# A hybrid encoder layer on one core: where near-key attention, residual sums and norm products are done

## The chip, the cores and the metric

One core of a Trainium2 chip runs the whole program. TensorE (PE in the profile; PEld its weight loads) multiplies, VectorE (DVE), ScalarE (ACT) and GpSimd (POOL) work element by element, and SyncE (SP) issues nearly all DMA transfers from one queue, in order. Every engine runs its own instructions in program order and waits on semaphores for the others. The metric is the device time of the program in microseconds; a profiled execution also gives a trace of every instruction. This kernel's runs differ by about 0.3%.

## The reference

One inference step of an encoder layer for 2048 prompt positions and 32 sample positions with a cache of 2048. Cut to what matters:

```python
h = rms_norm(x, g_norm1) * (1 + scale1) + shift1
q, k, v, z, xbc_raw, dt_raw = split(h @ w_in)
attn = stick_breaking(q, k, v)            # 8 heads: weights are beta_j times the product of
attn = rms_norm(attn, g_attn_out)         # (1 - beta) over the keys between j and the query
ssm = ssd_mixer(z, xbc_raw, dt_raw, ...)  # conv, SiLU, chunked scan, rms_norm
x = x + gate1 * (concat([attn, ssm]) @ w_out)
h2 = rms_norm(x, g_norm2) * (1 + scale2) + shift2
x = x + gate2 * ((silu(h2 @ w_gate) * (h2 @ w_up)) @ w_down)
```

with d_model 1024, FFN width 2816, all in float32. Further outputs are keys, values, and the final conv and scan states of prompt and sample.

## The kernel before

Every float32 product is made of two float32r halves, so a matrix is split into a high and a low part (`split`: ScalarE copies, another engine subtracts), and each block takes three matmuls (`mm3`, lines 130 to 132). Weights come by DMA in 1 MB tiles; ScalarE makes `wh`, GpSimd makes `wl`. `Pieces` fetches and splits one tile ahead of its use.

The 2048 positions go in four quarters of 512. The first phase (to about 985 us) projects them, runs the scan, and beside the last projection runs the attention of quarter 0 (`attn`). `scan` is its core: two sigmoids on ScalarE, masks on GpSimd, a running product on VectorE (`tensor_tensor_scan`), and the product `bv` with it (line 237), whose result TensorE transposes. At the end of that phase `ssm_out` and `conv_out` transpose the states, copy them and store them.

The second phase has `Wout`, the output projection of a quarter: `ssm()` adds the mixer's half, `run()` loads the attention's result (`rows`, from `aoD`), multiplies, and for each block of 128 rows makes the second norm (`norm2`). `product` scales the PSUM result by the row's rstd and the gate into `tm` (line 761) and adds it to `x1` (line 763); ScalarE then sums squares of `x1`. `norm2` takes the power -1/2 on GpSimd, scales `xn` on VectorE, transposes it on TensorE, applies scale and shift to the half blocks `hx` (hf 0 on ScalarE, four copies; hf 1 on VectorE, two operations), splits them into two-deep buffers `hl`, and stores these to `h2D`, from where the FFN of that quarter loads its input `h`.

Attention of quarters 1 to 3 looks at near keys only (`attn_w`, 8 heads a quarter, two scans a head); the few queries whose product has not vanished by then are redone over all far keys (`far_keys`).

The order is made by generators, whose yields carry a cost in ns. `merge2(main, side, ratio)` runs the main one and takes from the side one until its costs reach ratio times the main's. `merge2(w0.run(), a1, R2, fin=False)` so puts attention of quarter 1 beside the projection of quarter 0. Then `merge(streamA(), streamF(), 1.9)` interleaves two streams: A does the rest of the near-key attention, the far keys, and projections 1, 2, sample and 3; F does the FFN of the four quarters, in pieces of 96 gate and up matmuls and 48 down matmuls (`pg`, `pu`, `py`). For each cost unit of A, 1.9 of F are taken, and 4.0 once projection 1 is done. F may not load quarter g's input before A has yielded `("done", g)`. A scheduler in the build then moves instructions within this order where it expects engines to wait; what came out of it is shown with the change.

Tile names: `Q`, `Kw`, `Vw` are loads of `attn_w`, `z` scores or a projection's PSUM, `t` transposes, `o` attention results, `ao` an attention result on its way to or from `aoD`, `d` the PSUM of projection 0.

Of the kernel before, what the change touches and what calls it, by code (L numbers as in the profile page):

```python
# [9 lines left out]
AF = mybir.ActivationFunctionType  # L10
ALU = mybir.AluOpType
# [4 lines left out]
P = 128  # L16
# [9 lines left out]
SQ = 1  # L26
EPS = 1e-6
BIG = -1e30
R1, R2 = 1.6, 0.5
T2 = 4  # L30
CC = 3
NE = 4
# [3 lines left out]
def body(tc, nc, I, O):  # L36
    V, A, G, PE = nc.vector, nc.scalar, nc.gpsimd, nc.tensor
    ctx = ExitStack()
    with ctx:
# [169 lines left out]
        def scan(at_, aT, z, n, dd, first, end, mask, ns=2):  # L209

            a = aT[acnt[0] % len(aT)]
            acnt[0] += 1
            nb = abuf[0]
            b = at_.tile([P, 2, 256], F32, tag="b", name="b", bufs=nb)
            bv = b[:, :ns, :n]
            A.activation(a[:, :ns, 256 - n:256], z, AF.Sigmoid, scale=-1.0)
            A.activation(bv, z, AF.Sigmoid)
            av = a[:, :ns, 256 - n:256]
            if mask is not None:
                pat, np_ = mask  # L220
                for p0 in range(0, P, np_):
                    for t, fill in ((av, 1.0), (bv, 0.0)):
                        t = t[p0:p0 + np_]
                        G.affine_select(out=t, in_=t, pattern=pat, compare_op=ALU.is_gt, fill=fill, base=0, channel_multiplier=1)
            if first:
                V.memset(dd[:, :, 256:257], 1.0)
            Pt = at_.tile([P, 2, 257], F32, tag="P", name="Pt", bufs=2)
            if n == 256:
                fl = lambda t: t.rearrange("p a b -> p (a b)")[:, ::-1]
                V.tensor_tensor_scan(fl(Pt), fl(a), fl(dd), 0.0, op0=ALU.mult, op1=ALU.add)  # L230
            else:
                for i in range(ns):
                    r = lambda t: t[:, i, 256 - n:257][:, ::-1]
                    V.tensor_tensor_scan(r(Pt), r(a), r(dd), 0.0, op0=ALU.mult, op1=ALU.add)
            if not end:
                V.tensor_copy(dd[:, :ns, 256:257], Pt[:, :ns, 256 - n:257 - n])
            V.tensor_tensor(bv, bv, Pt[:, :ns, 257 - n:257], op=ALU.mult)
            return b

        def sums(stat, sq, hp, n):  # L240
# [476 lines left out]
        class Wout:  # L717
# [30 lines left out]
            def product(self, hf, r):  # L748

                mH, mL = mHL  # L750
                wh, wl = self.pf.get()
                for b, c, m in self.tb:
                    ps = self.psum()
                    tm = self.tile("tm", "tm")
                    if self.s == 0:
                        mm3(ps[:m], [(mH[:, k, c:c + m], mL[:, k, c:c + m], wh[:, k, :], wl[:, k, :]) for k in range(4)])
                    else:
                        mm2(ps[:2 * DEC], [(mH[:, k, :2 * DEC], wh[:, k, :], wl[:, k, :]) for k in range(4)])
                        fold(tm, ps, 512)
                        ps = tm  # L760
                    V.scalar_tensor_tensor(tm[:m], ps[:m], r[:m, b:b + 1], self.gr[hf][:m], op0=ALU.mult, op1=ALU.mult)
                    x1 = self.x1[hf, b]
                    V.tensor_tensor(x1[:m], x1[:m], tm[:m], op=ALU.add)
                    yield b, tm
                    yield 12 * 216

# [42 lines left out]
            def norm2(self, b, c, m):  # L809
                s, t0 = self.s, self.t0  # L810
                xs = [self.x1[hf, b] for hf in range(2)]
                ss = self.ss[b]
                V.tensor_tensor(ss[:m, 0:1], ss[:m, 0:1], ss[:m, 1:2], op=ALU.add)
                rs = sm.tile([P, 1], F32, tag="rsd", name="rsd")
                rstd(rs[:m], ss[:m, 0:1], 1.0 / D, EPS)
                xn = [self.tile("xn", "xn") for _ in range(2)]
                for hf in range(2):
                    V.tensor_scalar(xn[hf][:m], xs[hf][:m], rs[:m], None, op0=ALU.mult)
                    store(x1D[t0 + c:t0 + c + m, hf * 512:(hf + 1) * 512], xs[hf][:m])
                yield 1300  # L820
                for hf in range(2):
                    ps = tps()
                    pv = ps[:, :4 * m].rearrange("p (k t) -> p k t", k=4)
                    for k in range(4):
                        PE.transpose(pv[:, k, :], xn[hf][:m, k * P:(k + 1) * P], ident[:m, :m])
                    v4 = lambda t: t.rearrange("p (k t) -> p k t", k=4)[:, :, :m]
                    hx = v4(self.tile("tm", "hx"))
                    ksl = slice(hf * 4, hf * 4 + 4)
                    if hf == 0:
                        for k in range(4):  # L830
                            A.activation(hx[:, k, :], pv[:, k, :], AF.Identity, scale=A2[:, k, s:s + 1], bias=mods[:, 24 + k, s:s + 1])
                    else:
                        V.tensor_tensor(hx, pv, A2[:, ksl, s:s + 1].to_broadcast([P, 4, m]), op=ALU.mult)
                        V.tensor_tensor(hx, hx, mods[:, 24 + hf * 4:28 + hf * 4, s:s + 1].to_broadcast([P, 4, m]), op=ALU.add)
                    hl = [v4(self.tile(x, "hl", F32R)) for x in ("hh", "ll")]
                    split(hl[0], hl[1], hx)
                    for i in range(2):
                        store(h2D[i, ksl, :, t0 + c:t0 + c + m].rearrange("k p t -> p k t"), hl[i].bitcast(F32))
                    yield 450
# [205 lines left out]
        with ExitStack() as pa:  # L1045
# [525 lines left out]
            merge2(pr(2, "xz"), rest, 0.6, fin=False)  # L1571
            merge2(pr(2, "qv"), ssd_q(2), 0.68)
            merge2(chain(make_h(3, hH, hL), pr(3, "xz")), rest, 0.6)
            merge2(pr(3, "k"), ssd_q(3), 1.2)
            q = 3
            while klag:
# [5 lines left out]
            V.tensor_copy(mrT[:96], ps[:96, :P])  # L1582
            store(modD.rearrange("m s c -> (m s) c"), mrT[:96])
            ssm_out(st["S"], O["ssm_prompt"])
            ssm_out(st["Sx"], O["ssm_sample"])
            conv_out(carry, O["conv_prompt"])
            conv_out(sconv, O["conv_sample"])
            pr_.close()


# [11 lines left out]
        with ExitStack() as pb_:  # L1602
            mp = pb_.enter_context(tc.tile_pool(name="mp", bufs=1))
            mHL, stat = mixed(mp)
            pw0 = ExitStack()
            w0 = Wout(0, pw0.enter_context(tc.tile_pool(name="wo0", bufs=1)), dense_ps)
            w0.pre()
            merge2(a0, w0.ssm(), R1)
            pa0.close()
            fc = px_.enter_context(tc.tile_pool(name="fc", bufs=1, side="right"))  # L1610
            far_consts(fc)
            L = fc.tile([P, NH, 12], F32, name="L")
            px1 = ExitStack()
            at1 = px1.enter_context(tc.tile_pool(name="at1", bufs=1, side="right"))
            wt = window_tiles(at1)
            a1 = chain(*(attn_w(g, at1, L, wt) for g in range(1, NQ)))
            merge2(w0.run(), a1, R2, fin=False)
            pw0.close()
            fp = pb_.enter_context(tc.tile_pool(name="fp", bufs=1))
            late = {}  # L1620

            def streamA():
                yield from a1
                yield from far_keys(at1, wt[0], L)
                px1.close()
                for g in range(1, NQ):
                    if g == 3:
                        yield from part_s()
                    with tc.tile_pool(name=f"wo{g}", bufs=1, side="right") as wo:
                        yield from project(g, wo)  # L1630
                    if g < 3:
                        yield ("done", g)
                    if g == 1:
                        yield ("ratio", 4.0)
                px_.close()
                late["ex"] = pb_.enter_context(tc.tile_pool(name="ex", bufs=1, side="right"))
                dpool[0] = pb_.enter_context(tc.tile_pool(name="pdF", bufs=5, space=PSUM))
                yield ("done", 3)

            def streamF():  # L1640
                hT = load_h(0, fp, None)
                for g in range(NQ):
                    hT = yield from ffn(g, fp, late, hT)

            merge(streamA(), streamF(), 1.9)


        fx = ctx.enter_context(tc.tile_pool(name="fx", bufs=1))
# [39 lines left out]
def merge2(main, side, ratio, fin=True):  # L1688

    debt = 0.0  # L1690
    for c in main:
        debt += c * ratio
        while side is not None and debt > 0:
            try:
                debt -= max(next(side), 1)
            except StopIteration:
                side = None
    if side is not None and fin:
        for _ in side:
            pass  # L1700
# [58 lines left out]
```

## Time and profile before

| | us |
|---|---|
| three runs | 2985.84, 2990.13, 2994.29 (median 2990.13) |
| the profiled execution, device time | 2991.05 |
| its span, first to last instruction | 2989.3 |
| TensorE busy | 2741.2 (92%) |
| VectorE busy | 1630.7 (55%) |
| GpSimd busy | 1437.8 (48%) |
| ScalarE busy | 1165.4 (39%) |
| DMA | 466.53 MB, mean 156 GB/s |

Busy is the union of an engine's instructions. Matmuls are pipelined: one of 512 columns is listed with 0.39 us, but the next may start 0.23 us later, so it is the steps between starts that count. The granted clock is 1 at 2.4 GHz and 0.5 at 1.2 GHz, and a mean in between tells how much of a stretch ran at which. A wait is given with the instruction after it, its length and what released it.

### The profile page before, as it was taken

To read this page: it belongs to the slowest core of one execution; us is meant where nothing else is said; L and a number is where in the kernel's file an instruction comes from. 1 tells how busy PE (TensorE), PEld (TensorE's weight loads), DVE (VectorE), ACT (ScalarE), POOL (GpSimd) and SP (SyncE) were. 2 spreads that over 40 slices of the span, in tenths; PEclk is the share of its full clock that TensorE was granted. 3 is DMA by queue.
4 is the path that set the end of the run, shared out by engine and by line. 5 is a ranking of instruction groups with operands and counts; after the bars stand their busy time and mean duration, and the time that the engine had idled before them with its cause. 6 is when DMAs were issued, how large, how long until landed. Compare 5 with 4: busy or idle time off the path is not lost.

```text
span 2989.3 us, 41722 instructions
## 1 busy us (share of the span) xinstructions
PE 2741.2 (92%) x15467; PEld 2344.7 (78%) x15467; DVE 1630.7 (55%) x2690; ACT 1165.4 (39%) x2465; POOL 1437.8 (48%) x1237
## 2 busy tenths in 40 slices
PE   6998998988868679998989799999999999999998
PEld 4887997887867668887768588777788778899997
DVE  6577586756567667853445535435634432333336
ACT  6456465545444445522124233323232322322221
POOL 4667566564643435543126233544533545644445
PEclk8999999999988779999989899999999999999999
DMA  8755654363467696647644824444733462422221
GB/s 266 232 160 156 192 172 125 106 198 93 126 177 228 174 267 174 182 132 206 208 156 146 270 91 146 141 137 128 253 116 113 123 199 90 145 90 89 87 85 65
DMA packets 415618, 466.53 MB, mean 156 GB/s; under 512 B 34191, under 2 KB 330991, under 8 KB 415406
## 3 DMA queue, kind: packets, MB, share of 16 engines
q1 hardware_dynamic: 414478, 463.61, 51.5%
q8 instruction: 124, 2.03, 0.3%
q14 instruction: 88, 0.72, 0.1%
q10 hardware_dynamic: 896, 0.14, 0.0%
q0 software_dynamic: 32, 0.03, 0.0%
HBM read 372.66 MB, written 91.04 MB: 155 GB/s over the span
## 4 chain that ended last, share of the span: by engine, by line
PE 57%; DMA 7%; DVE 6%; POOL 2%; issue 2%; ACT 1%; SPq 1%; DVEq 0%; ACTq 0%; POOLq 0%
PE pg L131 5%; PE pu L131 5%; PE pu L130 5%; PE pu L132 5%; PE pg L130 5%; PE pg L132 5%; PE py L130 5%; PE py L131 4%; PE py L132 4%; PE d L132 2%; PE d L130 2%; PE d L131 2%; DMA Kf<-KT 1%; PE z L131 1%; PE z L130 1%
## 5 line engine op out<-in xcount | busy, mean ns | idle before, releaser
L60 POOL TENSOR_TENSOR wl<-wr,wh 128x512 fp32r<-128x512 f32 x752 | 1018.6, 1386 | 1033.9 <-ACT wh L59 947.1
L59 ACT ACTIVATE wh<-wr 128x512 fp32r<-128x512 f32 x816 | 449.8, 620 | 518.6 <-PE py L132 103.5
L130 PE MATMUL d<-wh,hH 128*128 128x256 f32 (+2 forms) x1088 | 313.6, 288 | 20.4 <-ACT hH L59 13.4
L130 PE MATMUL pg<-h,wh 128*128 128x512 f32 (+1 forms) x880 | 312.2, 355 | 16.5 <-DMA h<-h2D 16.5
L130 PE MATMUL pu<-h,wh 128*128 128x512 f32 (+1 forms) x880 | 312.4, 355 | 7.1 <-DVE sg L955 7.1
L132 PE MATMUL d<-wh,hL 128*128 128x256 f32 (+2 forms) x1088 | 309.1, 285 | 7.6 <-POOL hL L60 7.6
L131 PE MATMUL pg<-h,wh 128*128 128x512 f32 (+1 forms) x880 | 310.9, 353 | 1.6 <-DMA h<-h2D 1.6
L132 PE MATMUL pu<-h,wl 128*128 128x512 f32 (+1 forms) x880 | 311.7, 354 | 0.0
L131 PE MATMUL pu<-h,wh 128*128 128x512 f32 (+1 forms) x880 | 311.1, 354 | 0.0
L132 PE MATMUL pg<-h,wl 128*128 128x512 f32 (+1 forms) x880 | 310.7, 353 | 0.0
L131 PE MATMUL d<-wl,hH 128*128 128x256 f32 (+2 forms) x1088 | 308.6, 284 | 0.0
L130 PE MATMUL py<-wh,aH 128*128 128x512 f32 x704 | 285.1, 405 | 16.9 <-DVE ya L986 13.0
L131 PE MATMUL py<-wl,aH 128*128 128x512 f32 x704 | 280.0, 398 | 0.0
L132 PE MATMUL py<-wh,aL 128*128 128x512 f32 x704 | 268.6, 399 | 7.2 <-DVE aL L60 7.2
L986 DVE TENSOR_TENSOR ya<-py,ya 128x512 f32<-128x512 f32 x288 | 190.6, 685 | 127.7 <-PE py L132 125.3
L955 DVE TENSOR_TENSOR sg<-pg,sg 128x512 f32<-128x512 f32 (+1 forms) x110 | 64.9, 590 | 357.2 <-ACT sg L954 357.2
L130 PEld LDWEIGHTS d<-wh,hH 128*128 128x128 f32 (+1 forms) x1088 | 205.0, 188 | 24.4 <-ACT hH L59 14.9
L132 PEld LDWEIGHTS d<-wh,hL 128*128 128x128 f32 (+1 forms) x1088 | 204.3, 188 | 9.0 <-POOL hL L60 8.2
L131 PEld LDWEIGHTS d<-wl,hH 128*128 128x128 f32 (+1 forms) x1088 | 204.7, 188 | 0.9
L960 DVE TENSOR_TENSOR sg<-pu,sg 128x512 f32<-128x512 f32 (+1 forms) x110 | 65.0, 591 | 245.7 <-PE pu L132 244.4
L130 PEld LDWEIGHTS pg<-h,wh 128*128 128x128 f32 x880 | 166.1, 189 | 41.3 <-issue 15.9
L130 PEld LDWEIGHTS pu<-h,wh 128*128 128x128 f32 x880 | 166.5, 189 | 31.4 <-DVE sg L955 8.2
(435 smaller groups left out, 5758.1 us busy)
## 6 DMA issues: line engine op xcount, KB each, us to landing
wr<-in_w_in SPq DMA_DIRECT2D x48, 1024.0 KB
wr<-in_w_gate SPq DMA_DIRECT2D x44, 1024.0 KB
wr<-in_w_up SPq DMA_DIRECT2D x44, 1024.0 KB
wr<-in_w_down SPq DMA_DIRECT2D x44, 1024.0 KB
wr<-in_w_ada SPq DMA_DIRECT2D x24, 1024.0 KB
wr<-in_w_out SPq DMA_DIRECT2D x20, 1024.0 KB
h2D<-hl SPq DMA_DIRECT2D x64, 256.0 KB
Kw<-KT SPq DMA_DIRECT2D x48, 320.0 KB
```

Of the source, the lines that this page charges most:

```text
L59: A.activation(h, src, AF.Copy)
L60: (eng or V).tensor_tensor(l, src, h.bitcast(F32), op=ALU.subtract)
L130: PE.matmul(out, lhsT=sh, rhs=mh, start=(i == 0), stop=False)
L131: PE.matmul(out, lhsT=sh, rhs=ml, start=False, stop=False)
L132: PE.matmul(out, lhsT=sl, rhs=mh, start=False, stop=(i == n - 1))
L955: V.tensor_tensor(sg[:, :n], pg[:, :n], sg[:, :n], op=ALU.mult)
L960: V.tensor_tensor(sg[:, :n], pu[:, :n], sg[:, :n], op=ALU.mult)
L986: V.tensor_tensor(dst, ps[:r], dst, op=ALU.add)
```

## The change

Six edits. In `scan`, the last product goes to GpSimd in every other call. In `product`, the sum onto `x1` goes from VectorE to GpSimd. In `norm2`, ScalarE applies scale and shift to both half blocks. The sample's scan state and both conv states are put out before the key projection of quarter 3, not after it. Projection 0's `run()` is written alone, and the attention of quarter 1 is left to stream A. The ratio of the streams is 1.55 for 1.9 (until projection 1 is done; 4.0 after that stays).

```diff
-            V.tensor_tensor(bv, bv, Pt[:, :ns, 257 - n:257], op=ALU.mult)
+            (G if acnt[0] % 2 else V).tensor_tensor(bv, bv, Pt[:, :ns, 257 - n:257], op=ALU.mult)
...
-                    V.tensor_tensor(x1[:m], x1[:m], tm[:m], op=ALU.add)
+                    G.tensor_tensor(x1[:m], x1[:m], tm[:m], op=ALU.add)
...
-                    if hf == 0:
-                        for k in range(4):
-                            A.activation(hx[:, k, :], pv[:, k, :], AF.Identity, scale=A2[:, k, s:s + 1], bias=mods[:, 24 + k, s:s + 1])
-                    else:
-                        V.tensor_tensor(hx, pv, A2[:, ksl, s:s + 1].to_broadcast([P, 4, m]), op=ALU.mult)
-                        V.tensor_tensor(hx, hx, mods[:, 24 + hf * 4:28 + hf * 4, s:s + 1].to_broadcast([P, 4, m]), op=ALU.add)
+                    for k in range(4):
+                        kk = hf * 4 + k
+                        A.activation(hx[:, k, :], pv[:, k, :], AF.Identity, scale=A2[:, kk, s:s + 1], bias=mods[:, 24 + kk, s:s + 1])
...
+            ssm_out(st["Sx"], O["ssm_sample"])
+            conv_out(carry, O["conv_prompt"])
+            conv_out(sconv, O["conv_sample"])
             merge2(pr(3, "k"), ssd_q(3), 1.2)
...
             ssm_out(st["S"], O["ssm_prompt"])
-            ssm_out(st["Sx"], O["ssm_sample"])
-            conv_out(carry, O["conv_prompt"])
-            conv_out(sconv, O["conv_sample"])
...
-            merge2(w0.run(), a1, R2, fin=False)
+            run_all(w0.run())
...
-            merge(streamA(), streamF(), 1.9)
+            merge(streamA(), streamF(), 1.55)
```

What the build makes of it is shown at three places. First the queue of SP where quarter 0's last attention result (`aoD<-ao`) is stored and loaded again for the projection (`ao<-aoD`); `x2` counts equal neighbours. Before:

```order
L53 DMA wr<-in_w_down 128x2x1024
L56 DMA aoD<-ao 128x512
L53 DMA Q<-QT 64x512 x2
L53 DMA Kw<-KT 64x2x640 x2
L53 DMA Vw<-VS 128x5x128
L53 DMA ao<-aoD 128x512
```

The change:

```order
L53 DMA wr<-in_w_down 128x2x1024
L56 DMA aoD<-ao 128x512
L53 DMA ao<-aoD 128x512
L53 DMA Q<-QT 64x512 x2
L53 DMA Kw<-KT 64x2x640 x2
L53 DMA Vw<-VS 128x5x128
```

The load of the result has moved ahead of head 0's loads. Next TensorE between projection 0 and the first FFN matmul: the last transposes of the norm (`t<-ident,xn`) and what surrounds them. Before:

```order
L825 MATMUL t<-ident,xn 128x128 x4
L406 MATMUL o<-ll,Vw 128x128
L406 MATMUL o<-ll,Vw 128x256
L406 MATMUL o<-ll,Vw 128x128
L825 MATMUL t<-ident,xn 128x128 x8
L396 MATMUL t<-ident,b 128x128 x8
L406 MATMUL o<-hh,Vw 128x128
L406 MATMUL o<-hh,Vw 128x256
```

The change:

```order
L132 MATMUL d<-wh,mL 128x512
L371 MATMUL z<-Kw,Q 128x256 x4
L825 MATMUL t<-ident,xn 128x128 x32
L396 MATMUL t<-ident,b 128x128 x8
L406 MATMUL o<-hh,Vw 128x128
L406 MATMUL o<-hh,Vw 128x256
```

All 32 transposes now stand together behind the product; counted from the start of the attention of quarter 1 to the first `pg`, 9.5 heads' scores and 7 heads' results stood there before, and 4 heads' scores and 1 head's results stand there after. Last TensorE at the end of projection 1, with the last norm transposes, in the last FFN piece of quarter 0. Before:

```order
L132 MATMUL py<-wh,aL 128x512
L825 MATMUL t<-ident,xn 128x128 x8
L130 MATMUL py<-wh,aH 128x512
L131 MATMUL py<-wl,aH 128x512
L132 MATMUL py<-wh,aL 128x512
```

The change:

```order
L132 MATMUL pg<-h_11612,wl 128x512
L825 MATMUL t<-ident,xn 128x128 x8
L132 MATMUL pu<-h_11612,wl 128x512
L130 MATMUL pu<-h_11613,wh 128x512
L131 MATMUL pu<-h_11621,wh 128x512
```

Before, 12 down matmuls come behind these transposes and then the gate matmuls of quarter 1; in the change, 55 gate and up matmuls and 48 down matmuls of quarter 0 (with matmuls of projection 2 between them) come first.

## Rows read from the trace of the kernel before

**Rows 1.** Page: busy us and share of TensorE; its granted clock in 40 slices
```profile
PE 2741.2 (92%) x15467; PEld 2344.7 (78%) x15467; DVE 1630.7 (55%) x2690; ACT 1165.4 (39%) x2465; POOL 1437.8 (48%) x1237
...
PEclk8999999999988779999989899999999999999999
```

**Rows 2.** Stretches: length, busy us (instructions) per engine, TensorE clock, DMA share, GB/s
```profile
850.00:988.00 138.00, 109.82 (x607) 96.22 (x606) 103.46 (x172) 67.28 (x140) 41.75 (x39) 0.81 0.62 182
...
988.00:1097.00 109.00, 75.54 (x383) 66.19 (x382) 78.05 (x125) 52.72 (x109) 49.06 (x59) 0.72 0.97 261
...
1110.00:1266.00 156.00, 146.40 (x807) 125.23 (x806) 121.07 (x170) 82.95 (x154) 91.20 (x95) 0.97 0.67 177
...
1676.00:2560.00 884.00, 858.38 (x3726) 685.34 (x3727) 378.82 (x534) 282.40 (x539) 397.06 (x313) 0.99 0.45 142
```

**Rows 3.** Timeline of SP, 836 to 850 us: start, us, DMA issue
```profile
837.70 1.22 SPq L56 DMA_DIRECT2D out_ssm_sample<-so  x1
...
841.61 1.14 SPq L53 DMA_DIRECT2D Q<-QT  x2
```

**Rows 4.** Timeline of TensorE, same place; in brackets idle before it and releaser
```profile
844.20 1.11 PE L1219 MATMUL t<-ident,kn 128*128 128x128 f32 x4 [7.54 <-ACT co L1497]
```

**Rows 5.** Chain that ended last, 985 to 1106 us: start, us, what
```profile
987.91 1.99 DMA aoD<-ao
...
1001.15 0.64 ACT mH L59
...
1071.09 7.05 DMA h2D<-hl
```

**Rows 6.** Timeline of SP, 990 to 994 us
```profile
993.13 0.52 SPq L53 DMA_DIRECT2D ao<-aoD  x1
```

**Rows 7.** Timelines of VectorE, ScalarE, SP, TensorE, 1059 to 1096 us
```profile
1059.56 0.75 DVE L761 SCALAR_TENSOR_TENSOR tm<-d,ra,gr 128x512 f32<-128x512 f32 x1
...
1064.53 1.51 ACT L831 ACTIVATE hx<-t,mods,A 128x128 f32<-128x128 f32 x4
...
1068.63 10.68 SPq L56 DMA_DIRECT2D h2D<-hl  x8
...
1086.24 0.79 PE L130 MATMUL pg<-h,wh 128*128 128x512 f32 x1 [1.09 <-DMA h<-h2D]
...
1095.60 0.39 PE L131 MATMUL pg<-h,wh 128*128 128x512 f32 x1
...
1095.83 0.39 PE L132 MATMUL pg<-h,wl 128*128 128x512 f32 x1
```

**Rows 8.** Timeline of TensorE, 1003 to 1005 us
```profile
1003.70 0.63 PE L130 MATMUL d<-wh,mH 128*128 128x512 f32 x1
...
1004.13 0.63 PE L131 MATMUL d<-wl,mH 128*128 128x512 f32 x1
```

**Rows 9.** Groups of TensorE, 1110 to 1266: count, busy us, mean ns, idle
```profile
L130 PE MATMUL py<-wh,aH 128*128 128x512 f32 x48 | 19.8, 413 | 1.5 <-DVE sg L960 1.2 <-DVE ya L986 0.4
...
L130 PE MATMUL pu<-h,wh 128*128 128x512 f32 x43 | 17.3, 402 | 0.0
```

**Rows 10.** Timeline of TensorE, 1656 to 1677 us
```profile
1656.71 1.03 PE L825 MATMUL t<-ident,xn 128*128 128x128 f32 x8
...
1676.37 0.77 PE L130 MATMUL pg<-h,wh 128*128 128x512 f32 x1 [15.46 <-DMA h<-h2D]
```

**Rows 11.** Groups by line of VectorE, 1110 to 1266 us
```profile
L381 DVE TENSOR_TENSOR_SCAN Pt<-aT,dd 128x514 f32<-128x514 f32 x31 | 40.4, 1306 | 1.5 <-POOL aT L378 1.3
...
L384 DVE TENSOR_TENSOR b<-b,Pt 128x512 f32<-128x512 f32 x31 | 22.2, 715 | 0.0
```

**Rows 12.** Groups by line of GpSimd and VectorE, 1500 to 2560 us
```profile
L926 POOL TENSOR_TENSOR ya<-ya,gr 128x512 f32<-128x512 f32 x24 | 32.7, 1377 | 14.2 <-DVE ya L986 14.2
...
L763 DVE TENSOR_TENSOR x<-x,tm 128x512 f32<-128x512 f32 (+1 forms) x52 | 50.7, 976 | 6.3 <-DMA x<-in_x_prompt 5.0 <-DMA x<-in_x_sample 0.2
```

**Rows 13.** Line 381 in the whole span: ns least/median/most, first and last start
```profile
L381 DVE TENSOR_TENSOR_SCAN Pt<-aT,dd x48: 1196/1220/2286, 1001.3 to 1265.4; 128x514 f32<-128x514 f32 x48
```

More of the change, by code (lines that the diff above doesn't have):

```diff
@@ L28 @@
 BIG = -1e30
-R1, R2 = 1.6, 0.5
+R1 = 1.6
 T2 = 4
```

## The prediction, made before the changed kernel ran

> **What bounds the kernel now.** I read the page first. TensorE is busy for 92% of the span, and the reader should see how evenly: no other engine comes near it, and the granted clock is at its upper level (2.4 GHz) nearly everywhere except in a trough around slices 12 to 15 [rows 1]. So the end is set by TensorE's work, which the change leaves alone, plus the time in which TensorE stands idle or runs at the lower level (1.2 GHz). A change that moves work between the other engines and reorders it can only move those losses. The table of stretches says where they are [rows 2]: 850 to 988 us (attention of quarter 0) has 109.8 us busy of 138 at a mean clock of 0.81; 988 to 1097 us (first output projection beside attention of quarter 1) has 75.5 of 109 at 0.72, with the DMA engines 97% busy; 1110 to 1266 us (rest of the near-key attention beside the FFN) 146.4 of 156 at 0.97; and 1676 to 2560 us 858.4 of 884 at 0.99. Last I read the waits inside the poor stretches, one by one, as they come below.
>
> **The change part by part.** All sums are against the profiled execution: span 2989.3 us, 2991.05 us with what lies around it, 0.9 above the median of 2990.13.
>
> *State stores moved ahead of quarter 3's attention projection.* On SP, the store of the sample's state at 837.70 and three conv stores stand ahead of the first loads of attention, which go out at 841.61: 3.9 us [rows 3]. TensorE stands 7.5 us there, until the conv copies on ScalarE have freed the PSUM banks [rows 4]. After the change only the prompt's state store is left in that place. I take 4 us, the shift of the loads; the bounds are 0 (a transfer on another queue position sets the start anyway) and 7.5 (the whole wait). At their new place the same 20 transposes, 5 copies and 5 stores stand in a well filled stretch; they cost between 0 and 4.6 us (20 x 0.23, the step of a wide matmul, below), taken 1. Net 3 less.
>
> *Projection 0 alone.* Today the last attention result of quarter 0 is stored, lands at 989.9 [rows 5], and is loaded again only at 993.13, since the loads of head 0 of quarter 1 stand ahead of it on SP [rows 6]; ScalarE then splits it at 1001.15, because its sigmoids stand ahead and wait for those loads [rows 5]. After, the load is next on SP: it can go at 989.9. The store of the same 256 KB took 2.0 us [rows 5]; I take 3 for the load, so the split is at about 993.5. The product is 96 matmuls. At the upper clock one starts every 0.23 us [rows 7], at the lower every 0.43 [rows 8]; 96 x 0.23 = 22 us, and as today the first 9 us run at the lower level, which costs some 4.5 more; the 24 half as wide score matmuls that still stand between cost 3 (0.12 each). The product thus ends at about 1023; today its last eviction is at 1059.56 [rows 7]. Then come eight half blocks of the norm, whose two-deep buffers wait for their stores: one takes 7.1 us to land [rows 5]. Four pairs, three waits of some 7.5 us (a split and its issue with the landing), put the last store at about 1050; today it is issued by 1079.3 [rows 7]. From there to the first FFN matmul it takes 6.9 us today (1086.24, [rows 7]), so 1057 after. ScalarE now makes all eight half blocks (1.5 us for four scaled copies, [rows 7]) where VectorE made four; 2.1 us of ScalarE with the split fit under each landing. In the streams it is the same trade with ScalarE 282 of 884 us busy [rows 2]: nothing, and if that cover failed, 13 halves of 1.5 us, 20 us. That is 29 us less. Bounds: 22 if the DMA engines decide (five heads' loads of 1.2 MB each, by the shapes in the code, are no longer ahead: 6 MB at the 261 GB/s of that stretch, [rows 2]), 38 if landings shorten with the emptier queues.
>
> *What this pushes back.* By the order, 9.5 heads' scores and 7 heads' results stand before the first FFN matmul today, and 4 and 1 after: 5.75 heads go into the FFN stretch. In 1110 to 1266 us some 15 heads run (31 scans, two a head, [rows 11]) beside 407 FFN matmuls (three rows of 48 and six of 43 or 44, [rows 9]). TensorE's 156 us there less 9.6 idle [rows 2] less 407 x 0.23 is 53 us, 3.5 us a head. So 20 us come back: the gain of the projection is 9 us net, not 29.
>
> *The ratio 1.55.* Today the last norm transposes of projection 1 are at 1656.71, behind nearly all of the last FFN piece of quarter 0, and the FFN of quarter 1 then stands 15.5 us for its input [rows 10]. In the new order 55 gate and up matmuls and 48 down matmuls come behind those transposes: 103 x 0.23 = 24 us of cover for two transfers of some 7 us each and the issues of 16 loads. I take the whole wait, with 2 us of slow clock behind it: 17.5 less. Bounds: 10 (the last block's sum now stands behind residual products on GpSimd) and 18.
>
> *The longer attention stretch.* A head costs VectorE two scans of 1.31 and two products of 0.72 us [rows 11], and two splits and a sum about as long as a product: 6.2 us, some 6.9 with the small copies. In 1110 to 1266 that is 103 of its 121 us, which leaves the FFN 18 us for 2.8 pieces of 144 matmuls. By the order, 20 heads now stand beside the first 3.8 pieces instead of 14.5 beside 3.3, and the results reach into 4.3; with 20 x 6.9 + 4.2 x 6.4 = 165 us against TensorE's 20 x 3.5 + 4.2 x 33 = 209, VectorE is 79% busy, as now. I take 3 for waits that grow with it and 3 for the far-key loads, which come a little closer together: 6 more; between 0 and 20.
>
> *Sums and products on GpSimd.* A like sum on GpSimd takes 1.38 us; on VectorE it took 0.98 in the streams [rows 12]. 52 sums in the streams and 16 in projection 0 add 1.38 us each to GpSimd, 45% busy in 1676 to 2560 [rows 2], where it splits FFN weights a piece ahead; that lookahead hides them. If it fails, weights come late. VectorE gives up 51 us there, of which TensorE can feel only the few us it waits for VectorE. I take 3 more for late sums and 3 less for the freed VectorE: zero, between -8 and +15. In quarter 0's attention 12 or 13 of 26 products move; a longer product (1.4 us against 0.7) against an engine that is 103 of 138 us busy [rows 2]: 2 less, between -8 and +8.
>
> Beside this stands a rule. The scan, which reads two tiles of SBUF, takes 1.20 us at best and up to 2.29 [rows 13]: something blocks it at times. The Trainium skill, "SBUF — State Buffer", section "Who interferes with whom", says that a VectorE instruction with two SBUF inputs and a GpSimd instruction that reads SBUF exclude each other for the whole instruction; "Perfetto Trace Analysis", section "Optimizing Scalar/DVE Operations", adds that offloading between the two might not help. The trace agrees as far as the scan's spread goes. By that rule the moved work holds VectorE's two-input instructions for 1.38 instead of 0.7 us, and what it gives is rival B.
>
> **The sum.** 2991.0 - 3 - 29 + 20 - 17.5 + 6 + 0 - 2 = 2965.5; on the median's footing 2965.
>
> **The rivals.** *A: the startup is bound by transfers, and the input of quarter 1 is late again.* The projection gains its lower bound, 22, against 20 pushed back, and the wait at 1676 shrinks by 5 only: 2991 - 3 - 2 - 5 + 6 - 2 = 2985, no change. For it: the DMA engines at 97% in 988 to 1097. Against: the new order has 24 us of cover. *B: GpSimd's added reads slow VectorE until it is the bound of the attention stretch.* If the 40 scans there go from their mean of 1.31 to the 2.29 seen at worst [rows 11, 13], VectorE has 165 + 39 = 204 us against TensorE's 209, and with its waits on others half of that lands on the path: 20 more, 2985. For it: scans are stretched already. Against: few of the moved instructions stand in that stretch, and idle TensorE there is 6% only. *C, the other side: sums hold up the weight splits.* GpSimd runs in order, and in the order of the change two to seven sums stand in a row ahead of a weight split, each waiting for a product of TensorE. When GpSimd is 0.5 us late per sum beyond the lookahead, the 52 sums eat the forecast gain; at 0.8 us each, 42 us, it is 3007. The break is where a run of sums with its waits exceeds the time of one FFN weight tile, some 11 us; eight sums of 1.38 are 11.0 us, so it is near. Against: the order has weight splits between most sums, and GpSimd is half idle. *D: the change does not do what it says*, as the attention is hoisted back beside the projection: the order shows four heads' scores there, counted above; no more is possible.
>
> **How the numbers follow.** Forecast 0.64 (2945 to 2980). A 0.12 and B 0.10 (2981 to 2990), C 0.11 (2995 to 3015), a larger gain 0.03 (below 2945). A difference of 0.3%, 9 us, is about what a measurement of this kernel can tell from no change. Faster than 2981: 0.64 and 0.03 and a little of B, 0.68; within 2981 to 2999: 0.21; slower: 0.11. The range from 2942 to 2992 leaves out C and the larger gain.
>
> **What would show it.** Right: the first FFN matmul comes 25 to 35 us earlier than 1086.2, the 15.5 us wait of the first gate matmul of quarter 1 is gone, no 7.5 us wait at the seam near 840, and the stretch of near-key attention is longer by about 20 to 30 us. Wrong: new waits of weight splits on the sums (GpSimd idle before its sums, TensorE idle before gate or up matmuls), TensorE idle for over 10% of the attention stretch, or an FFN start no earlier than 1075.

## The result, and the profile after

The changed kernel takes 2939.84 us (2938.84 to 2944.78, four runs) against 2989.36 (2985.84 to 2994.29, four): ratio 0.9826, 95% interval 0.9811 to 0.9840. That is 50 us less by the medians and 52 by the ratio, where 25 were forecast and 2942 was the low end of the range. A later comparison of the same two gave 0.9838 (0.9820 to 0.9856). The profiled execution took 2940.34, its span is 2938.4.

The page of the changed kernel, beside [rows 1]: TensorE has lost 11 us of busy time, VectorE 67, GpSimd has gained 95.

```profile
PE 2729.8 (93%) x15467; PEld 2334.2 (79%) x15467; DVE 1563.9 (53%) x2575; ACT 1186.0 (40%) x2533; POOL 1532.6 (52%) x1318
...
PEclk8999998999988789999989999999999999999999
```

The same four stretches as [rows 2] (length, busy us and instructions of PE, PEld, DVE, ACT, POOL, clock, DMA share, GB/s):

```profile
850.00:988.00 138.00, 110.33 (x616) 95.80 (x616) 101.59 (x160) 67.60 (x142) 70.85 (x72) 0.83 0.70 202
988.00:1097.00 109.00, 80.48 (x384) 67.06 (x385) 64.29 (x87) 55.97 (x121) 53.64 (x55) 0.80 0.88 242
1110.00:1266.00 156.00, 151.98 (x883) 130.79 (x882) 134.62 (x191) 86.29 (x160) 101.96 (x102) 1.00 0.80 201
1676.00:2560.00 884.00, 872.63 (x3924) 701.86 (x3923) 333.94 (x497) 306.46 (x605) 458.03 (x366) 1.00 0.45 145
```

The start of the FFN has come forward from 1086.24 [rows 7] to 1048.26. Timeline of TensorE in the changed kernel, projection 0 (start, us, operation, in brackets idle before it and releaser):

```profile
1035.58 1.94 PE L825 MATMUL t<-ident,xn 128*128 128x128 f32 x8 [9.39 <-DVE xn L818]
...
1048.26 0.77 PE L130 MATMUL pg<-h,wh 128*128 128x512 f32 x1 [2.50 <-POOL aT L378]
```

The wait of 15.46 us before the first gate matmul of quarter 1 [rows 10] is gone; the same place after, where it follows a matmul of projection 2 without a gap:

```profile
1663.41 0.40 PE L131 MATMUL z<-wl,mH 128*128 128x512 f32 x1
1663.64 0.39 PE L130 MATMUL pg<-h,wh 128*128 128x512 f32 x1
```

At the seam, the wait for the conv copies [rows 4] is gone, but attention does not start earlier. TensorE before, then after:

```profile
849.33 0.55 PE L290 MATMUL z<-K,Q 128*128 128x256 f32 x1 [4.01 <-DMA Vt<-VS]
```

```profile
837.36 0.63 PE L1216 MATMUL t<-ident,kn 128*128 128x128 f32 x4 [2.15 <-DVE qhl L60]
839.60 0.58 PE L130 MATMUL d<-wh,hH 128*128 128x256 f32 x1 [1.61 <-ACT sq L1314]
...
850.78 0.55 PE L290 MATMUL z<-K,Q 128*128 128x256 f32 x1 [6.62 <-DMA K<-KT]
```

What had not been expected is in quarters 1 and 2. The waits of TensorE from 1676 to 2560 us (us in total, times, longest), before:

```profile
PE py L130 <- DVE ya L986: 12.3, 7, 3.6
PE pu L130 <- DVE sg L955: 5.8, 2, 4.9
PE py L132 <- DVE aL L60: 2.5, 3, 1.3
```

and after:

```profile
PE py L130 <- DVE ya L983: 3.0, 6, 1.0
PE py L132 <- DVE aL L60: 2.0, 2, 1.0
PE pu L130 <- DVE sg L952: 1.2, 1, 1.2
```

`ya` is the running sum of the FFN's output; it frees the PSUM bank that the next down matmul wants. Before, 20.6 us of waiting for VectorE stand in these three lines; after, 6.2. TensorE is busy for 14.2 us more of the same 884 us (872.63 against 858.38 [rows 2]).

### The profile page after: what moved, and what is told of

The parts are those of the page before. It is cut to its first block, busy times and chain, and to the rows that moved or that the text cites. A ratio compares the mean times of both kernels' runs of the same rounds, so it can differ in the third digit from the quotient of the medians.

```text
span 2938.4 us, 41844 instructions
## 1 busy us (share of the span) xinstructions
PE 2729.8 (93%) x15467; PEld 2334.2 (79%) x15467; DVE 1563.9 (53%) x2575; ACT 1186.0 (40%) x2533; POOL 1532.6 (52%) x1318
## 4 chain that ended last, share of the span: by engine, by line
PE 57%; DVE 6%; DMA 5%; issue 3%; POOL 2%; ACT 2%; SPq 1%; DVEq 0%; ACTq 0%; POOLq 0%
PE pg L130 5%; PE pg L131 5%; PE pg L132 5%; PE pu L130 5%; PE pu L131 5%; PE pu L132 5%; PE py L130 5%; PE py L131 4%; PE py L132 4%; PE z L130 2%; PE z L131 2%; PE z L132 1%; PE d L131 1%; PE d L130 1%; PE d L132 1%
## 5 line engine op out<-in xcount | busy, mean ns | idle before, releaser
L132 PEld LDWEIGHTS pg<-h,wl 128*128 128x128 f32 x880 | 165.4, 188 | 24.1 <-POOL wl L60 1.1
```

Of the source, the lines that this page charges most:

```text
L132: PE.matmul(out, lhsT=sl, rhs=mh, start=False, stop=(i == n - 1))
```

## The experiments

One number is common to all: the ratio to the kernel before, run on the same chip, where 0.001 is 3 us and intervals reach some 0.0013 to 0.003 to each side. Single runs of one kernel in one comparison spread by 2 to 20 us. Much of it comes at the start: the first `pyT` transposes, with the same program up to there, come at 261.8 us in one profiled execution and at 271.9 in another. The two profiled executions of the changed kernel differ by 15 us, of which 6.6 stand already there (264.4 and 271.0). So edits worth 5 us are at the edge of what these runs can tell. A second caution: the build's scheduler orders instructions by what it expects of the engines, so putting an operation back on VectorE also shifts some matmuls.

**Order and engines apart.** Order only: the changed kernel with the three engine moves undone. Engines only: the kernel before with the three moves.

```diff
-            (G if acnt[0] % 2 else V).tensor_tensor(bv, bv, Pt[:, :ns, 257 - n:257], op=ALU.mult)
+            V.tensor_tensor(bv, bv, Pt[:, :ns, 257 - n:257], op=ALU.mult)
...
-                    G.tensor_tensor(x1[:m], x1[:m], tm[:m], op=ALU.add)
+                    V.tensor_tensor(x1[:m], x1[:m], tm[:m], op=ALU.add)
...
(and the norm's second half on VectorE, as before)
```

> The changed kernel with its three engine moves undone: sums onto x, all products behind the scan and the second half of the norm are on VectorE again; only the order of the change is left (projection 0 alone, ratio 1.55, state stores ahead). The changed kernel takes 2939.8 us, the kernel before 2989.4. Theory O (the order gives it all, the engine moves nothing, as the prediction's sum has them): 2937 to 2945. Theory V (the 25 us that the forecast lacks come from a VectorE that has less to do in quarters 1 and 2): about 2965, and the waits of down matmuls for sums of VectorE (12.3 us in 1676 to 2560 before, 3.0 after) are back.

> The kernel before with the three engine moves alone; order, ratio 1.9 and stores stay as before. Theory O: 2984 to 2990, and the wait of 15.5 us at the first gate matmul of quarter 1 stays. Theory V: about 2965, the waits for sums of VectorE in quarters 1 and 2 gone though the order is that of before.

Order only: 2964.46, ratio 0.9898 (0.9881 to 0.9915). Engines only: 2975.37, 0.9941 (0.9925 to 0.9958). So the order gives 30 us, of 23.5 in the prediction's sum, and the engine moves 18 in the old order and about 20 in the new one, where the sum had 2. Theory O falls; theory V holds, if not to the full 25. In the engines-only kernel the wait at the first gate matmul of quarter 1 stays (12.49 us), so its 18 us come from elsewhere. In the order-only kernel the waits for VectorE from 1676 to 2560 us are back:

```profile
PE py L130 <- DVE ya L986: 12.8, 10, 3.7
PE t L825 <- DVE xn L818: 6.5, 3, 6.1
PE py L132 <- DVE aL L60: 3.6, 4, 1.3
```

**The two edits of order.** Ratio 1.9 for 1.55, and attention of quarter 1 beside projection 0 again, each in the changed kernel.

```diff
-            merge(streamA(), streamF(), 1.55)
+            merge(streamA(), streamF(), 1.9)
```

> The changed kernel with the ratio of the two streams at 1.9 again. By the prediction's step the ratio alone is worth 17.5 us (10 to 18): 2957 (2950 to 2958), with a wait of 10 to 16 us of the first gate matmul of quarter 1 for its input. If the ratio also buys the gain inside quarters 1 and 2 (the attention's stream further ahead, theory A): 2970 to 2985. If projection 0 alone and the lighter VectorE have made the ratio needless: 2938 to 2945.

Measured: 2962.47, 0.9884 (0.9853 to 0.9914), so the ratio is worth about 16 us (9 to each side by this run's interval), near the 17.5 of the sum. More than half of the wait is back:

```profile
1658.52 0.79 PE L130 MATMUL pg<-h,wh 128*128 128x512 f32 x1 [8.97 <-DMA h<-h2D]
```

```diff
-            run_all(w0.run())
+            merge2(w0.run(), a1, 0.5, fin=False)
```

> The changed kernel with attention of quarter 1 beside projection 0 again (ratio 0.5 as before); all else as changed. The traces have the first FFN matmul 38 us earlier and about 12 us of it given back before the far keys: if that is the worth of the step, 2966 (2960 to 2970), first FFN matmul at about 1085. If the heads that run beside the projection only change places with waits (nothing net, the prediction's lower bound of 22 against 20): 2938 to 2945.

Measured: 2939.66, 0.9821 (0.9800 to 0.9842): no different from the changed kernel. The first FFN matmul is 32 us later again,

```profile
1080.70 0.47 PE L130 MATMUL pg<-h,wh 128*128 128x512 f32 x1 [0.47 <-issue]
```

and it does not matter, because the heads that ran beside the projection are then missing from the later stretches: 17 of the 48 scans stand before the first FFN matmul here, 6 in the changed kernel. The first gate matmul of quarter 1 comes 14.5 us later than in the changed kernel and that of quarter 2 comes 22 us later, but that of quarter 3 comes at 2517.0 for 2518.1. The start of the FFN is a milestone that moved, not a gain.

**The engine moves one by one.** Each is undone alone in the changed kernel.

> The changed kernel with the sums onto x on VectorE again, all else as changed. The three engine moves together are worth 24.6 us (2964.5 without them). Theory S (the sums carry it: each reads two SBUF tiles and stands on VectorE ahead of what TensorE waits for): 2955 to 2962. Theory N (the norm's half carries it): 2940 to 2946. By the prediction's step (sums on GpSimd worth nothing, between -8 and +15): 2925 to 2948.

> The changed kernel with the second half of the norm (a product and a sum of 512 columns) on VectorE again, all else as changed. Theory N (the norm's half carries the 24.6 us, as two instructions of VectorE of 1.8 us together per block become part of ScalarE's idle time): 2955 to 2962, and the waits of norm transposes for VectorE longer at 1023 and 1038. Theory S: 2940 to 2946. By the prediction (nothing while ScalarE covers it): 2938 to 2943.

> The changed kernel with all products behind the scan in quarter 0's attention on VectorE again. The prediction takes 2 us for the move, between 8 gained and 8 lost: 2942, between 2932 and 2948. Seen in the trace of the changed kernel, two transposes there wait for the products of GpSimd (2.5 and 2.8 us at 890.9 and 919.3): a rival says that the move loses these, 2935.

Sums on VectorE: 2949.10, 0.9848 (0.9835 to 0.9862). Norm's second half on VectorE: 2959.66, 0.9887 (0.9871 to 0.9903). Products on VectorE: 2954.17, 0.9874 (0.9855 to 0.9892). Against the mean of the two comparisons of the changed kernel, 0.9832, that is 5, 16 and 13 us, each with some 6 to either side. The 13 can't be the products alone: sums and products together cost 9 (below), and in the profile 5 of the 13 stand already before attention begins (856.1 us against 850.8). From there to the first FFN matmul, where the products stand, it takes 200.0 us with them on VectorE and 197.5 and 197.9 in the two profiles of the changed kernel, so what they are worth is lost in the spread. The norm's half is the one that counts most. With it on VectorE, TensorE waits from 1676 to 2560 us:

```profile
PE py L130 <- DVE ya L986: 12.5, 10, 3.7
PE py L132 <- DVE aL L60: 3.6, 4, 1.3
```

The longest of these in the same kernel, on VectorE, GpSimd and TensorE in turn:

```profile
1818.62 1.76 DVE L834 TENSOR_TENSOR hx<-hx,mods 128x512 f32<-128x512 f32 x1
1820.30 1.76 DVE L60 TENSOR_TENSOR aL<-sg,aH 128x512 fp32r<-128x512 f32 x1
1821.99 3.44 DVE L60 TENSOR_TENSOR hl<-hx,hl 128x512 fp32r<-128x512 f32 x2
...
1826.01 1.87 DVE L986 TENSOR_TENSOR ya<-py,ya 128x512 f32<-128x512 f32 x3
```

```profile
1815.68 5.84 POOL L60 TENSOR_TENSOR wl<-wr,wh 128x512 fp32r<-128x512 f32 x4 [0.49 <-ACT wh L59]
1821.70 4.86 POOL L60 TENSOR_TENSOR wl<-wr,wh 128x512 fp32r<-128x512 f32 x3 [0.18 <-ACT wh L59]
```

```profile
1826.74 0.79 PE L130 MATMUL py<-wh,aH 128*128 128x512 f32 x1 [3.65 <-DVE ya L986]
```

Four instructions that take some 0.69 us each elsewhere take 1.72 to 1.76 here, while GpSimd splits weights; the three sums that free PSUM (1.87 us together) stand behind them. On ScalarE the first of them is out of that queue.

**Time on VectorE, or collisions?** The same half on VectorE, but as instructions that read PSUM and two columns of factors; first each done twice, then once.

```diff
+                            for _ in range(2):
+                                V.tensor_scalar(hx[:, k, :], pv[:, k, :], A2[:, kk, s:s + 1], mods[:, 24 + kk, s:s + 1], op0=ALU.mult, op1=ALU.add)
```

> The changed kernel with the norm's second half on VectorE, but as four instructions of 128 columns that read PSUM and two columns of factors, in place of a product and then a sum that reads two tiles of SBUF; and each done twice, so that VectorE spends about as long on it as on the old pair (1.8 us) or longer. Theory X (the old sum waits for GpSimd, since both read SBUF tiles, and delays what TensorE waits for): most of the 17 us is back, 2940 to 2949, no wait of 3.65 us of a down matmul near 1827 and 2284. Theory Y (any 1.8 us of VectorE in that place cost as much): 2955 to 2962 and these waits stay.

> The changed kernel with the norm's second half on VectorE as four instructions of 128 columns that read PSUM and two columns of factors, each once. In the run with each done twice one took 0.40 us whether GpSimd was busy or not, so the four are 1.6 us of VectorE, against 1.8 of the old pair, which costs 17 us. Theory X (what costs is that the old sum and the instructions behind it collide with GpSimd's reads of SBUF): 2942 to 2949. Theory Y (any 1.6 us of VectorE in that place cost as much): 2955 to 2962.

Twice: 2956.72, 0.9879 (0.9862 to 0.9897). Once: 2954.86, 0.9862 (0.9840 to 0.9884). Lines by duration (ns least/median/most): the new form is never stretched, while the old sum and the FFN's sum, the one with two tiles in SBUF and the other with one in PSUM, show the difference in the kernel before:

```profile
L835 DVE TENSOR_SCALAR hx<-t,A,mods x104: 290/402/414, 1583.5 to 2330.5; 128x128 f32<-128x128 f32 x96, 128x32 f32<-128x32 f32 x8
```

```profile
L834 DVE TENSOR_TENSOR hx<-hx,mods x13: 278/684/1784, 1628.4 to 2395.0; 128x512 f32<-128x512 f32 x12, 128x128 f32<-128x128 f32 x1
```

```profile
L986 DVE TENSOR_TENSOR ya<-py,ya x232: 628/690/694, 1545.4 to 2938.2; 128x512 f32<-128x512 f32 x116
```

Four of the new form in a row overlap and take 1.36 us, not 1.6. The old pair takes as long (0.68 and 0.68) where its sum isn't stretched, and 2.46 where it is, as in six of the 13 blocks of the kernel before. The once variant costs 9 us, the twice variant 14, the old pair 16. Neither theory's numbers come out: without the collision about half is back, within intervals that overlap. Nor does the sign that theory X named go with the time. The long waits for `ya` from 1676 to 2560 us are gone in the twice variant and there in the once variant; each line is of one profiled execution, twice and then once:

```profile
PE py L130 <- DVE ya L987: 2.8, 8, 0.8
```

```profile
PE py L130 <- DVE ya L987: 10.9, 9, 3.5
```

VectorE's time in that place costs something by itself; how much of the rest is the collision stays open, and the waits for `ya` alone do not price it.

**The norm's half alone.** On the kernel before, and in the new order without the other two moves.

> The kernel before with the norm's second half on ScalarE alone. All three engine moves in the old order gave 17.6 us. Theory N (the norm's half carries them): 2977 to 2983 on the footing of 2995. If it needs the other two as well: 2987 to 2996.

> The changed kernel with sums and all products on VectorE again: order and the norm's move alone. Order alone took 2964.5, the changed kernel 2940 to 2947. Theory N: 2944 to 2951. If sums and products carry the larger part: 2954 to 2963.

On the kernel before: 2979.32, 0.9945 (0.9927 to 0.9964), that is 16 us, all but 1 of what the three moves gave there. In the new order: 2956.95, 0.9861 (0.9837 to 0.9884), 11 us of 20, and 9 for sums and products together. The time itself lies in the range named for sums and products, on a footing of 2998 instead of 2994.5; with intervals of 7 us to either side the run can't tell which part is the larger. So the norm's half carries the gain in the old order and about half of it in the new one.

One share of the sums can be seen. In all six traces with the sums on VectorE TensorE waits once between 2030 and 2130 us for 4.8 to 6.1 us, behind an instruction of VectorE on 32 rows that stands for over 11 us (see the last section); in the fourteen with the sums on GpSimd no wait there is over 3.8. In the run with the sums alone on VectorE, which cost 5 us:

```profile
2070.88 0.63 PE L825 MATMUL t<-ident,xn 32*128 32x32 f32 x4 [6.14 <-DVE xn L818]
```

**The seam.** The stores put back in the changed kernel, and moved alone in the kernel before.

> The changed kernel with the sample's state store and the three conv stores back at the seam. The prediction gives the step 3 us (between 7.5 gained and 4.6 lost): 2943, a wait of 7.5 us near 844 for the conv copies of ScalarE. The rival, since the first score matmul of attention stands no earlier after the change (850.8 against 849.3) and now waits 6.6 us for its keys: the wait only moves, 2938 to 2942.

> The kernel before with the state stores moved alone. The prediction has 3 us less, between 7.5 less and 4.6 more: 2992 on this chip's footing of 2994.7. If the 12 us by which the changed kernel with the stores put back was longer are the seam's own: 2983. If they come of what stands behind it in the new order: 2990 to 2995.

Put back: 2954.62, 0.9869 (0.9853 to 0.9884). Moved alone: 2980.62, 0.9958 (0.9942 to 0.9973). Both say 11 to 13 us, four times the forecast. The changed kernel itself, beside the second of these runs, is the footing for both:

> The changed kernel itself, run beside the others as their footing, since the kernel before took 2994.7 us in the runs so far and 2989.4 in those of the first comparison. All theories: ratio 0.9826 (0.981 to 0.984) to the kernel before, 2940 to 2946. If it is 2950 or more, the 12 us each of the scan's products and of the stores were the footing, not the edits.

It came at 2946.77, 0.9838 (0.9820 to 0.9856), so a few us of the first difference are the footing; some 8 to 13 remain. Where they are: with the stores back, TensorE stands 7.38 us at 845.20, as before;

```profile
845.20 1.12 PE L1216 MATMUL t<-ident,kn 128*128 128x128 f32 x4 [7.38 <-ACT co L1494]
```

moved, 24 more matmuls of quarter 3's projection, some 4.5 us, come before the first score matmul (192 follow it, 216 with the stores at the seam). But with the stores back 5.5 us of the loss stand at the first FFN matmul and 12.9 only at the first gate matmul of quarter 1; and in the profile of the stores moved alone (2992.02 us, the slowest of its five, already 10 us late at the first `pyT`) most of the gain appears only beside projection 0. The place is not settled.

**Beyond both kernels.** Three further edits of the changed kernel: attention beside projection 0 with a larger cost (9000 for 3000) on the far-key sums; the norm's scaling `xn` on ScalarE; and combinations.

```diff
-                    V.tensor_scalar(xn[hf][:m], xs[hf][:m], rs[:m], None, op0=ALU.mult)
+                    A.activation(xn[hf][:m], xs[hf][:m], AF.Identity, scale=rs[:m])
```

> The changed kernel with attention beside projection 0 again (worth nothing by its own run) and a larger cost put on the far-key sums, 9000 for 3000, so that FFN matmuls stand between them. In the changed kernel there is no FFN matmul from 1460 to 1500 us, TensorE idles 19 of these 40 us and its clock falls to the lower level. Theory H (this hole is real loss): 20 to 30 us less, less some 5 for a later input of quarter 1, 2915 to 2930. Theory P (FFN work only changes places, since later stretches are as well filled without it): 2935 to 2945.

> The changed kernel with the norm's scaling of x (two tiles a block) on ScalarE too. On VectorE it took 0.48 us with GpSimd idle and up to 1.60 beside it, and four norm transposes of projection 0 wait for it. Theory X (an instruction that collides with GpSimd is worth moving to ScalarE, which waits for neither): 2930 to 2940. If VectorE has enough room by now: 2941 to 2948. If ScalarE, which squares, copies and splits the same blocks, is the late one now: 2950 to 2960.

> The changed kernel with attention beside projection 0 again and the norm's scaling of x on ScalarE. Alone the first gave ratio 0.9821, the second 0.9819, the changed kernel 0.9826 and 0.9838. If each is worth the 3 or 4 us that its run shows and they add: ratio 0.979 to 0.9805, some 2937 on the footing of 2998. If what they showed is the spread of the runs: 0.982 to 0.984.

> The same as in the run with attention beside projection 0 and the scaling on ScalarE, with the larger cost on the far-key sums too (9000 for 3000), so that FFN matmuls fill them. Its gain was nothing where VectorE did the scaling, and the product of projection 1 then waited 12 us for VectorE. If VectorE was what took it back, the lighter VectorE gives 5 us or more over the run without the larger cost; if FFN work only changes places, the two are equal within 3 us.

Ratios in that order: 0.9821 (0.9801 to 0.9840), 0.9819 (0.9795 to 0.9843), 0.9849 (0.9826 to 0.9871), 0.9825 (0.9800 to 0.9850). None differs from the changed kernel beyond its interval. Attention beside projection 0 alone (0.9821, above) and the scaling on ScalarE each looked 3 us better, and together they took 0.9849. The larger cost on top of both gave 7 us by the ratio, over the 5 that its text had named for VectorE; the intervals overlap, so this stays open. The hole was filled, as the stretch 1430 to 1530 us shows in the changed kernel and then in the one with the larger cost:

```profile
1430.00:1530.00 100.00, 77.99 (x294) 59.08 (x295) 41.20 (x66) 16.48 (x31) 26.39 (x20) 0.81 0.56 181
```

```profile
1430.00:1530.00 100.00, 85.44 (x364) 67.06 (x362) 47.09 (x75) 23.18 (x41) 25.74 (x20) 0.91 0.51 172
```

but the product of projection 1 then waits longer for VectorE (8.00 us in the changed kernel, at 1496.08):

```profile
1492.13 0.80 PE L130 MATMUL z<-wh,mH 128*128 128x512 f32 x1 [12.04 <-DVE tm L761]
```

and FFN matmuls used there are missing later. Against the run with attention beside projection 0 and the old cost, the first gate matmul of quarter 1 comes 24 us earlier (1654.4 for 1678.1) and that of quarter 3 only 3 (2513.9 for 2517.0): theory P.

## Why the prediction was wrong

- **Engine moves: the step that failed.** The sum had 2 us for all three; they are worth 18 in the old order and about 20 in the new. For the norm's half it priced only ScalarE (nothing, or 20 us lost without cover) and gave nothing for what VectorE is rid of. The paragraph on the sums did speak of "the few us it waits for VectorE" and took 3, without the row. The view of waits has it: 20.6 us in that very stretch, 6.2 after. That was the term to write down, with 20 us as its upper end; 14 of it went, as much as TensorE was busy longer there. That the three moves lighten VectorE and that TensorE waits less for it is shown; how the gain of the norm's half divides between a shorter queue and fewer collisions is not. The clock follows: from 0.99 [rows 2] to 1.00 in 884 us.
- **The rule, read for the wrong side.** The runs bear out the Trainium skill, "SBUF — State Buffer", section "Who interferes with whom": a sum with one input in PSUM took 0.69 us whatever GpSimd did, one with two in SBUF up to 1.78. The prediction took it as a danger of the moved sums (rival B). But those are collisions that exist already, and a sum or a product taken off VectorE ends one; what that is worth the runs leave open. Rival B did not happen: in 1110 to 1266 us TensorE is busier than before, and the scans went from a mean of 1.31 us [rows 11] to 1.39, not to 2.29:

```profile
L381 DVE TENSOR_TENSOR_SCAN Pt<-aT,dd 128x514 f32<-128x514 f32 x33 | 45.6, 1387 | 2.6 <-POOL aT L378 2.4
```

- **Seam: mis-sized.** 3 was forecast, at most 7.5; 8 to 13 is what the runs show. The shift of the loads was the wrong measure: loads went out 2.8 us earlier (838.80 for 841.61) and the first score matmul came no earlier. What changed there is which work is done before it; where the gain arises is not settled.
- **Projection 0 alone, with what it pushes back and the longer stretch: net right.** Minus 29, plus 20, plus 6 is 3 us less; the run without the edit says 0, within its interval of 6. The parts were off: the FFN starts 38 us earlier, the upper bound, and all of it is given back, more than the 20. The last scan starts at 1262.1 us, for 1265.4 [rows 13], so the near-key attention behind the first FFN matmul is 35 us longer, where 20 to 30 were named.
- **Ratio: right.** 17.5 forecast, about 16 by its own run, and the wait is gone as said. With that and the FFN's earlier start, rival A did not happen.
- **Sums holding up weight splits (rival C): did not happen.** The longest wait of TensorE for a weight from 1676 to 2560 us is 1.2 us.
- The order's terms add to 23.5 less in the sum and 30 in the run, and the engine moves to 2 and 20: together the 25 us that the forecast was short.

## What to carry to other kernels

Before an edit that unloads an engine is priced at nothing because that engine is half idle, add up what the bound engine waits for it, from the view of waits of the stretch: an in-order engine at 43% busy was still late 12 times. That sum is an upper estimate and not a price: in the once and twice variants the time did not follow it. An earlier milestone is no gain by itself when two streams share the bound engine; ask what work is no longer there later. And where GpSimd works in long rows, look first at the instructions of VectorE that read two tiles of SBUF, and test them: here such a sum took up to 1.78 us for 0.69, and ending that was worth some 7 us of 16, within intervals that overlap.

## What the runs showed of the hardware

VectorE can be shut out for much longer than one instruction of GpSimd. In the kernel before, a product of 32 by 512 that reads two tiles stands for 14.23 us, as long as GpSimd works without a pause. An up matmul then waits for the product `sg`; its sigmoid stands on ScalarE behind squares that need the sum made from this product. VectorE, GpSimd and TensorE there:

```profile
2094.68 14.23 DVE L761 SCALAR_TENSOR_TENSOR tm<-tm,ra,gr 32x512 f32<-32x512 f32 x1 [1.56 <-POOL ra L150]
```

```profile
2094.62 1.28 POOL L926 TENSOR_TENSOR ya<-ya,gr 128x512 f32<-128x512 f32 x1
2095.88 5.03 POOL L60 TENSOR_TENSOR wl<-wr,wh 128x512 fp32r<-128x512 f32 x4
2100.87 1.28 POOL L926 TENSOR_TENSOR ya<-ya,gr 128x512 f32<-128x512 f32 x1
2102.11 5.01 POOL L60 TENSOR_TENSOR wl<-wr,wh 128x512 fp32r<-128x512 f32 x4
2107.09 1.28 POOL L927 TENSOR_TENSOR ya<-ya,xf 128x512 f32<-128x512 f32 x1
```

```profile
2113.65 0.79 PE L130 MATMUL pu<-h,wh 128*128 128x512 f32 x1 [4.90 <-DVE sg L955]
```

The changed kernel has such a stand late in the last quarter, where TensorE does not wait for it; it ends when GpSimd pauses at 2909.1. The kernel before has the same at 2947.0, and 17 of the 20 traces have it with 13.3 or 13.4 us. In the second profile of the changed kernel a sum of 32 by 1 stands for 10.36 us. First the late stand, then this one:

```profile
2896.01 13.40 DVE L60 TENSOR_TENSOR aL<-sg,aH 128x272 fp32r<-128x272 f32 x1 [0.50 <-ACT aH L59]
```

```profile
2068.86 10.36 DVE L813 TENSOR_TENSOR s<-s 32x1 f32<-32x1 f32 x1 [1.16 <-ACT tm L852]
```

The Trainium skill, "SBUF — State Buffer", section "Summary: rules for kernel authors", has the engine that issues second wait until the first one's instruction is finished; here VectorE gets no turn between eleven of GpSimd's in a row. Elsewhere, as in the rows of the split at 1820, it gets its turn each time. What makes the difference was not tried. The shape alone does not: in the run with ratio 1.9 a split of 128 by 512 (`aL`) stood for 6.70 us. The scaling `xn`, with one tile of input, is stretched as well (least 470, median 486, most 1615 ns in the kernel before).
